# Pre-norm gains moved from the weights to the turned rows of a two-layer encoder, with queries scaled by 1/rms, two more raw weight buffers and one transfer for the constants

## The chip, the cores and the metric

The kernel runs on one core of a Trainium2 chip. The metric is the device time of one execution in microseconds (us). A core has five engines that work side by side and wait for each other by semaphores: TensorE (PE, matmuls and transposes), VectorE (DVE), ScalarE (ACT), GpSimd (POOL) and SyncE (SP, which here only issues transfers). Each takes its instructions in order.

## The reference, cut to what matters

512 rows of 1024 values pass two layers. Each layer is a token mixer with 12 query heads over 3 key/value heads, plus 4 heads that attend to 256 memory rows, then a SwiGLU network, with a norm ahead of and behind each half:

```python
def rms_norm(x, g):
    y = x * lax.rsqrt(jnp.mean(x * x, axis=-1, keepdims=True) + EPS)
    return y * g

mem_n = rms_norm(mem, mem_norm_g)
for i in range(2):
    h = rms_norm(x, g_mix_pre[i])
    proj = h @ w_in[i]                 # q (768), k (192), v (192), qm (256)
    # layer 0: window of +-128 tokens, a sink logit, rotary on 16 of 64 dims
    # layer 1: all 512 tokens; q = rope(rms_norm(q, qk_g[0])), k = rope(rms_norm(k, qk_g[1]))
    mkv = mem_n @ w_mem_kv[i]          # keys and values of the memory heads
    x = x + rms_norm(concat([tok, mo]) @ w_o[i], g_mix_post[i])
    h = rms_norm(x, g_ffn_pre[i])
    x = x + rms_norm((silu(gate) * up) @ w_down[i], g_ffn_post[i])
```

The gain `g` of a pre-norm has one value for each of the 1024 columns that a product sums over. It can be multiplied into the weights' rows, or into the activations.

## The kernel before

Everything is fp32. PE multiplies a rounded format, so every operand is split into a part `hi` and a rest `lo`, and a product is three matmuls (`mm3`, L239 to L243: hi·hi, then the two with a `lo`). `split` (L245) makes the two from a source: `hi` by ACT (or POOL, side bit 2), `lo` as source minus `hi` by DVE (or POOL, side bit 1). `split_scaled` (L257) does the same with a factor per partition.

Rows of x and of the memory are turned (transposed) by PE, so that the 1024 columns lie along the partitions: `turned` (L303) makes eight transposes of 128 x 128 into two PSUM tiles `tp` (a tag with two buffers) and splits each with one ACT and one DVE instruction of 512 columns into `hT` (x) or `mT` (memory). The factor 1/rms of a row isn't multiplied in there, but where a product is taken out of PSUM.

`unit` (L192) brings in a block of weights: a transfer into a raw buffer (`raw`, three of them), then the split, with the gain column `gcol` as the factor. There are four units of K/V weights `wkv` (768 columns), four of memory weights `wm` (1024), and per query group two of `wq` (1024). With `side` odd, POOL first multiplies `raw` by the gains in place (L214) and `split` follows; otherwise `split_scaled` does it in one go.

A mixer runs over K/V for the four row tiles (`kv_pieces`), memory keys and values (`mem_pieces`), four query groups (`q_pieces`), and then per head and row tile scores, exponentials, transposes of the probabilities and products with the values. In layer 1, `rope_b` (L398) norms keys and queries per head: squares, sum, `r` = 1/rms on POOL (L269, L270), the rotation on DVE (L414 to L416). Keys are multiplied by `r` ahead of the rotation (L409); for queries `r` is kept in `rq4` and applied later, as the scale of the exponential, for which DVE makes a bias `nb` = −max · r for every head and tile (L537). `start` (L1076) is the beginning of the program: constants, x, the four K/V units.

What sets the order: PE's is written out by hand, from a table of numbers per layer that places every piece on one axis (`put(x, f)`, L646). On the other engines and the queues a scheduler of the framework orders the instructions when the kernel is built. So PE's order is the same before and after the change, while that of ACT, DVE, POOL and SP is not.

Of the kernel before, what the change touches and what calls it, by code (L numbers as in the profile page):

```python
# [179 lines left out]
class Trunk:  # L180
    def __init__(self, tc, a):
        self.tc, self.nc, self.a = tc, tc.nc, a
# [9 lines left out]
    def unit(self, src, side=0, pool=None, parts=1, put=None, x=0, dst=None, key=None, g=None, raw=None):  # L192

# [4 lines left out]
        def load():  # L198
            raw = own or self.wraw.tile([P, 1024], F32, tag="raw", name="raw", bufs=3)
            hi, lo = [(pool or self.whl).tile([P, 1024], F32R, tag=z, name=f"w{z}", bufs=4) for z in ("hi", "lo")]  # L200
            if not own:
                nc.sync.dma_start(raw[:, :n], src)
            return raw, hi, lo

        def part(t, c0, c1):
            raw, hi, lo = t
            if g is None:
                self.split(hi[:, c0:c1], lo[:, c0:c1], raw[:, c0:c1], side)
                return
            m = n // g.shape[1]  # L210
            for k in range(c0 // m, c1 // m):
                c = slice(k * m, k * m + m)
                if side & 1:
                    nc.gpsimd.tensor_scalar(raw[:, c], raw[:, c], g[:, k:k + 1], 1.0, op0=OP.mult, op1=OP.mult)  # L214
# [42 lines left out]
    def split_scaled(self, hi, lo, src, r, pool=0):  # L257

        nc = self.nc
        if pool & 2:  # L260
            nc.gpsimd.tensor_scalar(hi, src, r, 1.0, op0=OP.mult, op1=OP.mult)
        else:
            nc.scalar.activation(hi, src, AF.Copy, scale=r)  # L263
        nc.vector.scalar_tensor_tensor(lo, src, r, hi.bitcast(F32), op0=OP.mult, op1=OP.subtract)  # L264
# [38 lines left out]
    def turned(self, h, his, los, t, nq=4):  # L303

        for b in range(2):
# [5 lines left out]
            self.split(his[k0 // nq][sl], los[k0 // nq][sl], tp)  # L311
# [30 lines left out]
    def mem_pieces(self, l, mk, put, x0, dx, lag, xw):  # L342

        w, ps = {}, []
        for u in range(4):
            self.unit(self.a["wm"][l, u], self.side(l, "mw", u), put=put, x=xw[u], dst=w, key=u,
                      g=self.gcol[:, DEPTH, 2 * u:2 * u + 2])
# [50 lines left out]
    def rope_b(self, x, t, n, z):  # L398
# [7 lines left out]
        r = self.small.tile([P, 4], F32, tag=f"r4{z}", name="r4", bufs=2 if z else 12)  # L406
        self.rstd(r[:, :n], ss[:, :n], HD)
        if z:
            v.tensor_mul(x[:, :n], x[:, :n], r[:, :n, None].to_broadcast([P, n, HD]))  # L409
# [7 lines left out]
        return r  # L417

    def rope(self, l, x, t, n, z):
        return self.rope_a(x, t, n) if l == 0 else self.rope_b(x, t, n, z)  # L420
# [40 lines left out]
    def q_pieces(self, l, c, qTs, put, x0, lead):  # L461
        nc = self.nc
        w = {}
        for z in range(2):
            self.unit(self.a["wq"][l, c, z], self.side(l, "qw", 2 * c + z), put=put, x=x0 - lead + z * lead / 3, dst=w,
                      key=z, g=self.gcol[:, l, 4 * z:4 * z + 4])

        def prod(t, st, u):
# [10 lines left out]
            if u == 3:  # L479
# [6 lines left out]
                if c < 3:  # L486
                    self.rq4[c, t] = self.rope(l, qx, t, 4, 0)
# [20 lines left out]
    def score(self, hd, i):  # L508
# [22 lines left out]
        else:  # L531
            nc.vector.tensor_reduce(nm[:, i:i + 1], s[:, :n], axis=AX.X, op=OP.max if hd["norm"] else OP.min)  # L532
        bias, scale = nm[:, i:i + 1], -1.0
        if hd["norm"]:
            r = self.rq4[hd["hg"] // 4, i][:, hd["hg"] % 4:hd["hg"] % 4 + 1]
            bias, scale = self.small.tile([P, 1], F32, tag="nb", name="nb", bufs=6), r
            nc.vector.tensor_scalar(bias, nm[:, i:i + 1], r, -1.0, op0=OP.mult, op1=OP.mult)  # L537
        nc.scalar.activation(p[:, :n], src[:, :n], AF.Exp, bias=bias, scale=scale, accum_out=den[:, i:i + 1])  # L538
# [72 lines left out]
    def consts(self, glob):  # L611
        nc, a = self.nc, self.a
        self.ropet = glob.tile([P, 2, NT, 16], F32, name="ropet")
        nc.gpsimd.dma_start(self.ropet.rearrange("p a t d -> p (a t d)"), a["ropea"])
        self.sink = glob.tile([P, NH], F32, name="sink")
        self.nsink = glob.tile([P, NH], F32, name="nsink")
        nc.gpsimd.dma_start(self.sink, _rows(a["attn_sink"], NH))
        self.gt = glob.tile([P, 2, 2, NT, HD], F32, name="gt")

    def axial(self, buf):  # L620
# [6 lines left out]
        nc.gpsimd.tensor_scalar(g[:, 0], g[:, 0], HD ** -0.5, 1.0, op0=OP.mult, op1=OP.mult)  # L627
# [7 lines left out]
    def mixer(self, l, mkp, late, tokp):  # L635
        nc = self.nc
        pc = PACE[l]
        if l == 0:
            self.mask = self.core.tile([P, 3 * P], F32, name="mask", tag="mask")
            nc.sync.dma_start(self.mask, self.a["mask"])  # L640
            nc.gpsimd.tensor_scalar(self.nsink, self.sink, -1.0, 1.0, op0=OP.mult, op1=OP.mult)
        self.pbufs = (3 * P, 15) if l == 0 else (4 * P, 12)
        qT, mk, items, count = {}, {}, [], itertools.count()
        self.rq4 = {}
# [22 lines left out]
        def heads():  # L667
            for hg in range(NH + NMH):
                c, h = divmod(hg, 4)
                hd = dict(hg=hg, norm=l == 1 and c < 3, q=lambda c=c, h=h: qT[c][:, h], sink=hg if l == 0 and c < 3 else None)  # L670
# [16 lines left out]

        k = pc["kstep"]
# [28 lines left out]
    def post_norm(self, t, og, y, e, ss, gn, resid, dst, rs, h=None):  # L717
# [17 lines left out]
        if rs is not None:  # L735
            self.factors(y, rs[:, t:t + 1], self.junk)
            return lambda: self.turned(h, *self.hT, t)
# [109 lines left out]
    def ffn_out(self, get, w, fs, o, head, gpost, resid, dst, rs):  # L847
# [25 lines left out]
        for t in range(NT):  # L873
# [5 lines left out]
            if rs is not None and t == NT - 1:  # L879
                self.wkv = [self.unit(self.a["wkv"][1, u], g=self.gcol[:, 1, 2 * u:2 * u + 2]) for u in range(4)]  # L880
# [195 lines left out]
    def start(self, mkp):  # L1076
# [3 lines left out]
        with ExitStack() as st:  # L1080
# [5 lines left out]
            nc.scalar.dma_start(ident, a["ident"])  # L1086
            self.consts(self.glob)
# [133 lines left out]
```

## Time and profile before

| | |
|---|---|
| median of 3 runs | 1134.27 us (1134.18 to 1135.16) |
| the profiled execution | 1132.73 us, its span 1131.0 us |
| granted TensorE clock, share of full speed | 0.998 |
| layer 0: K/V, memory and queries; heads | about 8 to 62 us; 63 to 180 us |
| layer 0: output of the mixer; network | to 222 us; to 537 us |
| layer 1: turning and mixer | about 555 to 745 us |
| layer 1: output of the mixer; network | to 790 us; to the end |

In the profile, a row of a timeline has the start, the duration, the engine, the line of the kernel, the operation, out<-in and shapes, how many, and in brackets the idle time ahead of it with what ended it. A row of a group has the busy us, the mean ns of one and the idle time ahead. "L255 DVE TENSOR_TENSOR hT<-tp,hT" is the `lo` part of a turned tile, for instance: the line is that of `split`, the tile tells whose it is.

### The profile page before, as it was taken

To read this page: it belongs to the slowest core of one execution; us is meant where nothing else is said; L and a number is where in the kernel's file an instruction comes from. 1 tells how busy PE (TensorE), PEld (TensorE's weight loads), DVE (VectorE), ACT (ScalarE), POOL (GpSimd) and SP (SyncE) were. 2 spreads that over 40 slices of the span, in tenths; PEclk is the share of its full clock that TensorE was granted. 3 is DMA by queue.
4 is the path that set the end of the run, shared out by engine and by line. 5 is a ranking of instruction groups with operands and counts; after the bars stand their busy time and mean duration, and the time that the engine had idled before them with its cause. 6 is when DMAs were issued, how large, how long until landed. Compare 5 with 4: busy or idle time off the path is not lost.

```text
span 1131.0 us, 19555 instructions
## 1 busy us (share of the span) xinstructions
PE 1102.3 (97%) x7463; PEld 1007.6 (89%) x7463; DVE 839.8 (74%) x1477; ACT 665.3 (59%) x1361; POOL 211.7 (19%) x370
## 2 busy tenths in 40 slices
PE   9999999999999999999999999999999999999997
PEld 7889988899889989998888888778999899899985
DVE  4788885899548857874688998758985478669854
ACT  6578984666335624553567998756654255345531
POOL 4693331102000000000327643312000000000001
PEclk9999999999999999999999999999999999999999
DMA  6521015433513332335532110145135123422243
GB/s 236 187 80 52 20 57 205 150 131 116 157 38 112 129 96 75 113 91 194 180 115 76 38 38 20 57 153 182 41 110 168 56 78 113 146 65 98 84 165 112
DMA packets 34141, 122.51 MB, mean 108 GB/s; under 512 B 3952, under 2 KB 4336, under 8 KB 33920
## 3 DMA queue, kind: packets, MB, share of 16 engines
q1 hardware_dynamic: 33696, 121.13, 32.4%
q8 instruction: 58, 0.95, 0.3%
q14 instruction: 35, 0.29, 0.1%
q0 software_dynamic: 64, 0.07, 0.1%
q10 hardware_dynamic: 288, 0.08, 0.0%
HBM read 110.77 MB, written 10.49 MB: 107 GB/s over the span
## 4 chain that ended last, share of the span: by engine, by line
PE 66%; DVE 7%; ACT 4%; POOL 2%; issue 2%; DMA 0%; POOLq 0%; DVEq 0%; ACTq 0%
PE ps L961 12%; PE ps L962 12%; PE ps L963 12%; PE ps L241 9%; PE ps L243 9%; PE ps L242 9%; PE tp L586 1%; DVE tl L255 1%; DVE wlo L264 1%; PE o L601 1%; DVE nm L532 1%; PE o L600 1%; ACT junk L274 1%; ACT p L538 1%; POOL p L576 1%
## 5 line engine op out<-in xcount | busy, mean ns | idle before, releaser
L251 ACT ACTIVATE whi<-raw 128x1024 fp32r<-128x1024 f32 (+1 forms) x176 | 148.2, 853 | 183.8 <-PE ps L963 95.8
L255 DVE TENSOR_TENSOR wlo<-raw,whi 128x1024 fp32r<-128x1024 f32 (+1 forms) x164 | 161.5, 991 | 70.6 <-ACT whi L251 70.5
L961 PE MATMUL ps<-sf,whi 128*128 128x256 f32 x640 | 180.5, 282 | 0.0
L963 PE MATMUL ps<-sf,whi 128*128 128x256 f32 x640 | 180.5, 282 | 0.0
L962 PE MATMUL ps<-sf,wlo 128*128 128x256 f32 x640 | 180.4, 282 | 0.0
L241 PE MATMUL ps<-whi,f 128*128 128x512 f32 x352 | 137.2, 390 | 0.0
L242 PE MATMUL ps<-wlo,f 128*128 128x512 f32 x352 | 137.2, 390 | 0.0
L243 PE MATMUL ps<-whi,f 128*128 128x512 f32 x352 | 137.0, 389 | 0.0
L962 PE MATMUL ps<-a,wlo 128*128 128x256 f32 x480 | 135.2, 282 | 0.0
L961 PE MATMUL ps<-a,whi 128*128 128x256 f32 x480 | 134.7, 281 | 0.0
L963 PE MATMUL ps<-a,whi 128*128 128x256 f32 x480 | 134.3, 280 | 0.0
L961 PEld LDWEIGHTS ps<-sf,whi 128*128 128x128 f32 x640 | 121.4, 190 | 0.9 <-ACT p L967 0.4
L962 PEld LDWEIGHTS ps<-sf,wlo 128*128 128x128 f32 x640 | 121.5, 190 | 0.5
L963 PEld LDWEIGHTS ps<-sf,whi 128*128 128x128 f32 x640 | 121.7, 190 | 0.0
L279 POOL TENSOR_SCALAR e<-sso 128x1 f32<-128x1 f32 x8 | 3.4, 423 | 568.9 <-ACT junk L274 568.7
L241 PE MATMUL ps<-whi,hT 128*128 128x256 f32 (+1 forms) x320 | 98.9, 309 | 0.9 <-ACT whi L263 0.9
L576 POOL TENSOR_SCALAR p<-p,rd 128x256 f32<-128x256 f32 (+2 forms) x128 | 76.8, 620 | 102.0 <-DVE rd L573 36.1
L242 PE MATMUL ps<-wlo,hT 128*128 128x256 f32 (+1 forms) x320 | 94.0, 294 | 1.0 <-DVE wlo L264 1.0
L243 PE MATMUL ps<-whi,hT 128*128 128x256 f32 (+1 forms) x320 | 93.5, 292 | 0.0
L963 PEld LDWEIGHTS ps<-a,whi 128*128 128x128 f32 x480 | 90.8, 189 | 0.0
L961 PEld LDWEIGHTS ps<-a,whi 128*128 128x128 f32 x480 | 90.6, 189 | 0.2
L962 PEld LDWEIGHTS ps<-a,wlo 128*128 128x128 f32 x480 | 90.5, 188 | 0.2
(205 smaller groups left out, 2780.5 us busy)
## 6 DMA issues: line engine op xcount, KB each, us to landing
raw<-in_wgu_dram SPq DMA_DIRECT2D x48, 512.0 KB, 4.4
raw<-in_wd_dram SPq DMA_DIRECT2D x44, 512.0 KB, 4.3
rb<-in_wgu_dram SPq DMA_DIRECT2D x40, 512.0 KB, 3.6
raw<-in_wq_dram SPq DMA_DIRECT2D x16, 512.0 KB, 3.7
raw<-in_wo_dram SPq DMA_DIRECT2D x16, 512.0 KB, 3.5
xt<-x SPq DMA_DIRECT2D x12, 512.0 KB, 4.5
raw<-in_wm_dram SPq DMA_DIRECT2D x8, 512.0 KB, 4.4
x<-y SPq DMA_DIRECT2D x8, 512.0 KB, 3.0
```

What stands on the lines that cost most here:

```text
L241: mm(out, lh, rh, start=first, stop=False)
L242: mm(out, lh, rl, start=False, stop=False)
L243: mm(out, ll, rh, start=False, stop=last)
L251: nc.scalar.activation(hi, src, AF.Copy)
L255: nc.vector.tensor_sub(lo, src, hi.bitcast(F32))
L264: nc.vector.scalar_tensor_tensor(lo, src, r, hi.bitcast(F32), op0=OP.mult, op1=OP.subtract)
L274: self.nc.scalar.activation(scratch, x, AF.Square, scale=D ** -0.5, accum_out=ss)
L532: nc.vector.tensor_reduce(nm[:, i:i + 1], s[:, :n], axis=AX.X, op=OP.max if hd["norm"] else OP.min)
L576: self.pooled = nc.gpsimd.tensor_scalar(hd["p"][z][:, :n], hd["p"][z][:, :n], rd[:, z:z + 1], 1.0, op0=OP.mult, op1=OP.mult)
L961: mm(out, wh[:, s], rh, start=start and k == 0, stop=False, skip_group_check=True)
L962: mm(out, wl[:, s], rh, start=False, stop=False, skip_group_check=True)
L963: mm(out, wh[:, s], rl, start=False, stop=k == 3, skip_group_check=True)
```

## The change

The gains are multiplied into the turned rows instead of the weights. Since after turning a column of x lies on a partition, but four of them side by side in one PSUM tile (each 128 rows wide), `turned` now splits each of the eight 128 x 128 squares by itself with `split_scaled`. Only the first tile of x is done otherwise: DVE multiplies 512 columns by a broadcast gain into a buffer, and `split` follows from there. Weights are split unscaled, in larger pieces (768 or 512 columns); POOL's scalings are gone.

In layer 1, queries are multiplied by `r` on DVE, behind the rotation (keys too, now), so the exponential's scale is −1 and its bias the score minimum `nm`; `nb` is gone. The sign is put into the query gain.

In the mixer of layer 1 two of every five raw loads use one of two new buffers (`raw2`). The identity, the rotary table of layer 0 and the gains come in one transfer `cst` on ACT's queue; the sink logits move from POOL's queue to SP's, behind x and the memory, and their negation moves into the mixer.

```diff
-    def unit(self, src, side=0, pool=None, parts=1, put=None, x=0, dst=None, key=None, g=None, raw=None):
+    def unit(self, src, side=0, pool=None, parts=1, put=None, x=0, dst=None, key=None, raw=None):
...
         def part(t, c0, c1):
             raw, hi, lo = t
-            if g is None:
-                self.split(hi[:, c0:c1], lo[:, c0:c1], raw[:, c0:c1], side)
-                return
-            m = n // g.shape[1]
-            for k in range(c0 // m, c1 // m):
-                c = slice(k * m, k * m + m)
-                if side & 1:
-                    nc.gpsimd.tensor_scalar(raw[:, c], raw[:, c], g[:, k:k + 1], 1.0, op0=OP.mult, op1=OP.mult)
-                else:
-                    self.split_scaled(hi[:, c], lo[:, c], raw[:, c], g[:, k:k + 1], side)
-            if side & 1:
-                self.split(hi[:, c0:c1], lo[:, c0:c1], raw[:, c0:c1], side)
+            self.split(hi[:, c0:c1], lo[:, c0:c1], raw[:, c0:c1], side)
...
+    def raw(self):
+
+        self.nraw += 1
+        if self.more and self.nraw % 5 in (1, 3):
+            return self.more.tile([P, 1024], F32, tag="raw2", name="raw", bufs=2)
+        return self.wraw.tile([P, 1024], F32, tag="raw", name="raw", bufs=3)
...
-    def turned(self, h, his, los, t, nq=4):
+    def turned(self, h, g, his, los, t, nq=4, buf=None):
...
-            self.split(his[k0 // nq][sl], los[k0 // nq][sl], tp)
+            hi, lo = his[k0 // nq][sl], los[k0 // nq][sl]
+            if buf is not None:
+                x = buf[:, 512 * b:512 * b + 512].rearrange("p (k n) -> p k n", n=P)
+                self.nc.vector.tensor_mul(x, tp, g[:, k0:k0 + 4, None].to_broadcast([P, 4, P]))
+                self.split(hi, lo, x)
+                continue
+            for k in range(4):
+                self.split_scaled(hi[:, k], lo[:, k], tp[:, k], g[:, k0 + k:k0 + k + 1])
...
-        if z:
-            v.tensor_mul(x[:, :n], x[:, :n], r[:, :n, None].to_broadcast([P, n, HD]))
         tmp = self.core.tile([P, 4, HD], F32, tag="rt", name="rt", bufs=2)
...
         v.tensor_add(x[:, :n], x[:, :n], tmp[:, :n])
-        return r
+        v.tensor_mul(x[:, :n], x[:, :n], r[:, :n, None].to_broadcast([P, n, HD]))
...
-            nc.vector.tensor_reduce(nm[:, i:i + 1], s[:, :n], axis=AX.X, op=OP.max if hd["norm"] else OP.min)
-        bias, scale = nm[:, i:i + 1], -1.0
-        if hd["norm"]:
-            r = self.rq4[hd["hg"] // 4, i][:, hd["hg"] % 4:hd["hg"] % 4 + 1]
-            bias, scale = self.small.tile([P, 1], F32, tag="nb", name="nb", bufs=6), r
-            nc.vector.tensor_scalar(bias, nm[:, i:i + 1], r, -1.0, op0=OP.mult, op1=OP.mult)
-        nc.scalar.activation(p[:, :n], src[:, :n], AF.Exp, bias=bias, scale=scale, accum_out=den[:, i:i + 1])
+            nc.vector.tensor_reduce(nm[:, i:i + 1], s[:, :n], axis=AX.X, op=OP.min)
+        nc.scalar.activation(p[:, :n], src[:, :n], AF.Exp, bias=nm[:, i:i + 1], scale=-1.0,
+                             accum_out=den[:, i:i + 1])
...
-            nc.scalar.dma_start(ident, a["ident"])
-            self.consts(self.glob)
-            nc.scalar.dma_start(gcol.rearrange("p z k -> p (z k)"), a["gcol"])
+            nc.scalar.dma_start(self.cst, a["cst"])
...
+            nc.sync.dma_start(self.sink, _rows(a["attn_sink"], NH))
```

How the order moves, at three places. First ACT in layer 0, at the memory tiles: `mT` is their `hi` part, `vs` and `kx` are values and keys of the last x tile on their way out of PSUM, `whi` weights. Before:

```order
L251 ACTIVATE whi<-raw 128x512 x4
L251 ACTIVATE mT<-tp 128x4x128 x2
L263 ACTIVATE vs<-ps,rs 128x3x64
L251 ACTIVATE mT<-tp 128x4x128
L263 ACTIVATE whi<-raw,gcol 128x256 x4
L444 ACTIVATE kx<-ps,rs 128x192
L251 ACTIVATE mT<-tp 128x4x128
```

After:

```order
L246 ACTIVATE whi<-raw 128x512 x4
L254 ACTIVATE mT<-tp,cst 128x128 x3
L254 ACTIVATE vs<-ps,rs 128x3x64
L254 ACTIVATE mT<-tp,cst 128x128 x2
L440 ACTIVATE kx<-ps,rs 128x192
L246 ACTIVATE whi<-raw 128x512 x2
L254 ACTIVATE mT<-tp,cst 128x128 x3
L246 ACTIVATE k_556<-kx 128x3x64
L254 ACTIVATE mT<-tp,cst 128x128 x8
```

The first memory tile had both its halves ahead of `vs`; now its eight pieces are spread around `vs`, `kx` and a weight unit, and the second tile's eight follow.

Second POOL in layer 0, from the end of the memory weights to the first normalised probabilities `p`. Before:

```order
L214 TENSOR_SCALAR raw<-raw,gcol 128x256 x8
L253 TENSOR_TENSOR wlo<-raw,whi 128x512 x2
L249 TENSOR_SCALAR whi<-raw 128x512 x2
L253 TENSOR_TENSOR wlo<-raw,whi 128x512 x2
L214 TENSOR_SCALAR raw<-raw,gcol 128x256 x3
L373 TENSOR_SCALAR k_821<-k_821 128x4x64
L214 TENSOR_SCALAR raw<-raw,gcol 128x256 x4
L249 TENSOR_SCALAR whi<-raw 128x512 x2
L373 TENSOR_SCALAR k_845<-k_845 128x4x64
L253 TENSOR_TENSOR wlo<-raw,whi 128x512 x2
L214 TENSOR_SCALAR raw<-raw,gcol 128x256 x5
L576 TENSOR_SCALAR p<-p,rd 128x256
```

After:

```order
L248 TENSOR_TENSOR wlo<-raw,whi 128x512 x4
L244 TENSOR_SCALAR whi<-raw 128x512 x2
L248 TENSOR_TENSOR wlo<-raw,whi 128x512 x2
L371 TENSOR_SCALAR k_851<-k_851 128x4x64
L244 TENSOR_SCALAR whi<-raw 128x512 x2
L371 TENSOR_SCALAR k_876<-k_876 128x4x64
L248 TENSOR_TENSOR wlo<-raw,whi 128x512 x2
L568 TENSOR_SCALAR p<-p,rd 128x256
```

Twenty scalings are gone, five of them directly ahead of `p`.

Third DVE in layer 1, at the first scores: `nm` is the score's extreme, `qx` a query tile in rotation. Before:

```order
L405 TENSOR_REDUCE ss_7461<-sq 128x4
L414 TENSOR_TENSOR rt<-qx,gt 128x4x32
L532 TENSOR_REDUCE nm<-s 128x1
L415 TENSOR_TENSOR qx<-qx,gt 128x256
L537 TENSOR_SCALAR nb<-nm,r_7196 128x1
L416 TENSOR_TENSOR qx<-qx,rt 128x256
L532 TENSOR_REDUCE nm<-s 128x1 x2
L537 TENSOR_SCALAR nb<-nm,r_7260 128x1
L537 TENSOR_SCALAR nb<-nm,r_7330 128x1
L255 TENSOR_TENSOR q_7472<-qx,q_7472 128x4x64
```

After:

```order
L403 TENSOR_REDUCE ss_7504<-sq 128x4
L410 TENSOR_TENSOR rt<-qx,gt 128x4x32
L528 TENSOR_REDUCE nm<-s 128x1
L411 TENSOR_TENSOR qx<-qx,gt 128x256
L528 TENSOR_REDUCE nm<-s 128x1
L412 TENSOR_TENSOR qx<-qx,rt 128x256
L528 TENSOR_REDUCE nm<-s 128x1
L413 TENSOR_TENSOR qx<-qx,r_7507 128x256
L528 TENSOR_REDUCE nm<-s 128x1
L250 TENSOR_TENSOR q_7516<-qx,q_7516 128x4x64
```

The small `nb` instructions are gone and a multiply of the query tile by `r` stands behind the rotation, with a score reduction and the query's `lo` part behind it.

More of the change, by code (lines that the diff above doesn't have):

```diff
@@ L198, in load @@
         def load():
-            raw = own or self.wraw.tile([P, 1024], F32, tag="raw", name="raw", bufs=3)
+            raw = own or self.raw()
             hi, lo = [(pool or self.whl).tile([P, 1024], F32R, tag=z, name=f"w{z}", bufs=4) for z in ("hi", "lo")]
@@ L345, in mem_pieces @@
         for u in range(4):
[L346 to L347 removed]
+            self.unit(self.a["wm"][l, u], self.side(l, "mw", u), put=put, x=xw[u], dst=w, key=u)
         def prod(u, m):
@@ L879, in ffn_out @@
             if rs is not None and t == NT - 1:
-                self.wkv = [self.unit(self.a["wkv"][1, u], g=self.gcol[:, 1, 2 * u:2 * u + 2]) for u in range(4)]
+                self.wkv = [self.unit(self.a["wkv"][1, u]) for u in range(4)]
             join(ps, t, 1)
@@ L1111, in factors @@
                                         op1=OP.mult)
-            self.turned(x[0], *self.hT, 0)
+            self.turned(x[0], gcol[:, 0], *self.hT, 0, buf=tmp.tile([P, D], F32, tag="buf", name="buf", bufs=1))
             busy(8)
```

57 lines of the change are left out of this document (26 added, 31 removed).

## The prediction

> **What bounds the kernel now.** I read the page first, then the waits of TensorE, then the timelines around each wait.
>
> ```profile
> span 1131.0 us, 19555 instructions
> PE 1102.3 (97%) x7463; PEld 1007.6 (89%) x7463; DVE 839.8 (74%) x1477; ACT 665.3 (59%) x1361; POOL 211.7 (19%) x370
> ```
>
> TensorE (PE) is busy 97% of the span, and neither the matmuls nor their order change. So the change is worth only what it takes from, or adds to, PE's stalls; busy time that it saves on DVE, ACT or POOL counts nowhere else. By the code it acts in the two mixers and in the turning ahead of them. The view of PE's waits, by what ended them, shows how little there is to win:
>
> ```profile
> PE tp L385 <- DVE kb L386: 2.4, 1, 2.4
> PE tp L586 <- POOL p L576: 2.0, 4, 0.9
> PE s L521 <- ACT p L538: 1.5, 2, 1.1
> PE tp L308 <- DVE mT L255: 0.9, 1, 0.9
> PE tp L586 <- DVE nb L537: 0.9, 2, 0.6
> PE o L600 <- DVE nb L537: 0.5, 1, 0.5
> ```
>
> (Columns: total us, times, longest.) These six rows together are 8.2 us, the size of the stake. Below, minus is faster.
>
> **Start of layer 0.** Four raw K/V weight units arrive, are split into hi and lo, and PE consumes them as they come:
>
> ```profile
> 9.85 1.12 ACT L263 ACTIVATE whi<-raw,gcol 128x384 fp32r<-128x384 f32 x2 [1.62 <-DMA raw<-in_wkv_dram]
> 10.51 0.45 PE L241 MATMUL ps<-whi,hT 128*128 128x384 f32 x1 [0.94 <-ACT whi L263]
> 14.28 1.03 PE L308 MATMUL tp<-ident,h 128*128 128x128 f32 x8
> ```
>
> ACT waited 1.62 us for a transfer, so the stage is set by the loads. Two software-queue transfers and one on ACT's queue go; that could let the raw units land earlier, by at most about that 1.62 us. Against it, a unit is now split in one piece of 768 instead of two of 384: with the two pieces taking 1.12 us together, PE's first matmul on a unit starts about 0.4 us later. The first x tile also makes a detour, two DVE multiplies into a buffer ahead of its split. I take **−0.3**, ends −1.0 and +0.8: the halves nearly cancel.
>
> **The turned rows in pieces.** This is what the change adds. A turned tile was two ACT and two DVE instructions of 512 columns; for the nine tiles after the first it becomes eight and eight of 128, each with its own gain column. No 128-column piece of this kind is in the trace; the nearest rows read PSUM with a per-partition scale, on ACT and on DVE:
>
> ```profile
> L251 ACT ACTIVATE hT<-tp 128x512 fp32r<-128x512 f32 x16 | 8.9, 594 | 3.6 <-PE tp L308 3.6
> L263 ACT ACTIVATE vs<-ps,rs 128x192 fp32r<-128x192 f32 x8 | 3.4, 420 | 2.7 <-PE ps L243 2.7
> L263 ACT ACTIVATE vm<-ps,rs 128x256 fp32r<-128x256 f32 x4 | 1.9, 474 | 1.3 <-DVE k L264 1.2
> L255 DVE TENSOR_TENSOR hT<-tp,hT 128x512 fp32r<-128x512 f32 x16 | 10.6, 687 | 9.0 <-ACT hT L251 8.9
> L264 DVE SCALAR_TENSOR_TENSOR vs<-ps,rs,vs 128x192 fp32r<-128x192 f32 x8 | 3.3, 411 | 0.9 <-ACT vs L263 0.7
> L264 DVE SCALAR_TENSOR_TENSOR vm<-ps,rs,vm 128x256 fp32r<-128x256 f32 x4 | 1.9, 480 | 1.6 <-ACT vm L263 1.6
> L444 ACT ACTIVATE kx<-ps,rs 128x192 f32<-128x192 f32 x8 | 3.4, 419 | 2.1 <-DVE vs L264 2.0
> ```
>
> Carrying 192 and 256 columns on to 128 gives an estimate of 0.37 us on ACT and 0.34 on DVE, so a tile takes 8 × 0.37 + 0.34 = 3.3 us from first to last instead of about 0.594 + 0.594 + 0.687 = 1.9. The last row warns of more: ACT's read of a PSUM tile waited for DVE's read of the same one, and in the changed order an ACT piece stands behind the DVE piece ahead of it, so both engines go in step and anything else queued between the pieces delays all that follow.
>
> The Trainium skill speaks against this step: "VectorE: DVE Perf Modes", section "The TRN2 errata — SBUF-src ops pay a fixed extra latency per instruction", says that every instruction pays a fixed latency and advises tiles of 512 elements or more. By its PSUM figure of 120 cycles at 0.96 GHz, an estimate for six more DVE pieces a tile is 0.75 us; the rows above agree in direction and give more, 8 × 0.34 − 2 × 0.69 = 1.3 us. With the page's price the three turning terms below (5.6 us) would shrink to some 3.2 and the sum to about −4.8, an estimate.
>
> What PE feels depends on the place.
>
> ```profile
> 15.55 1.29 DVE L255 TENSOR_TENSOR hT<-tp,hT 128x512 fp32r<-128x512 f32 x2 [0.71 <-ACT hT L251]
> 16.20 0.33 PE L241 MATMUL ps<-whi,hT 128*128 128x384 f32 x1
> 30.46 1.04 PE L308 MATMUL tp<-ident,mh 128*128 128x128 f32 x8
> 31.97 1.06 ACT L251 ACTIVATE mT<-tp 128x512 fp32r<-128x512 f32 x2
> 32.72 1.27 DVE L255 TENSOR_TENSOR mT<-tp,mT 128x512 fp32r<-128x512 f32 x2
> 33.45 1.25 PE L308 MATMUL tp<-ident,mh 128*128 128x128 f32 x8 [0.91 <-DVE mT L255]
> L274 ACT ACTIVATE scr<-h 128x512 f32<-128x512 f32 x8 | 5.0, 629 | 0.0
> ```
>
> Tile 1 of x is consumed the moment it is ready: PE begins on it at 16.20, as the first DVE half ends. PE takes some 0.5 us per column group (three matmuls of about 0.17), the pieces alone would keep up, but squares of 0.63 us and the value copy of 0.42 stand between them on ACT. Laid out in that order, the fourth column group is ready about 1.7 us after PE wants it; tiles 2 and 3 have a whole tile of products as cover. **+1.7**, ends +0.5 (squares slip into gaps) and +2.4.
>
> The memory tiles are worse. PE turns the second one at 33.45, already 0.91 us late, because it writes the PSUM tiles that the first one is still being read from. Now those come free only after pieces 7 and 8, with a value copy (0.42), a key copy and weight pieces queued between them: 31.6 for the transposes + 0.5, then 8 × 0.37 + 0.34 + 2 × 0.42 and about 1.3 of weight pieces, is 37.4. Before, the stall ended 3 us after the transposes began; now nearly 6. **+2.9**, ends +1.6 (nothing between the pieces) and +3.8 (DVE's weight pieces too).
>
> **POOL's scalings.** Each POOL-side weight unit was scaled in place first:
>
> ```profile
> L214 POOL TENSOR_SCALAR raw<-raw,gcol 128x256 f32<-128x256 f32 x36 | 18.0, 518 | 7.9 <-DMA raw<-in_wq_dram 7.8
> 69.78 2.35 POOL L214 TENSOR_SCALAR raw<-raw,gcol 128x256 f32<-128x256 f32 x5
> 72.11 2.23 POOL L576 TENSOR_SCALAR p<-p,rd 128x256 f32<-128x256 f32 x4
> 72.64 0.33 PE L586 MATMUL tp<-ident,p 128*128 128x128 f32 x1 [0.89 <-POOL p L576]
> ```
>
> At 72.64 PE waits for normalised probabilities (0.89, then 0.40 at the next), and they wait for five scalings that now are gone. Late next would be the exponentials, a little over 2 us earlier than POOL took them. **−1.8** with the slower pace of the transposes, ends −1.9 and −0.5.
>
> **Layer 1's turning.** The same pieces meet a tighter place: tile 2's transposes at 561.4 need the PSUM tiles of tile 1, and the K/V units stand among the pieces on ACT. **+1.0**, ends 0 (the 1.3 us of a tile lies beside products) and +2.3.
>
> **Layer 1's keys, queries and loads.**
>
> ```profile
> 582.01 0.73 ACT L263 ACTIVATE whi<-raw,gcol 128x512 fp32r<-128x512 f32 x1 [1.43 <-DMA raw<-in_wm_dram]
> 586.25 0.36 DVE L409 TENSOR_TENSOR kx<-kx,r 128x192 f32<-128x192 f32 x1 [1.03 <-POOL r L270]
> 587.52 0.55 DVE L386 CAST kb<-tp 128x384 fp32r<-128x384 f32 x1
> 588.22 0.43 PE L385 MATMUL tp<-identr,k 128*128 128x128 f32 x3 [2.38 <-DVE kb L386]
> 609.40 1.28 ACT L538 ACT_TABLE_LOAD   x1 [1.36 <-DVE nb L537]
> 611.62 0.50 PE L521 MATMUL s<-ka,qT 128*128 128x512 f32 x1 [1.09 <-ACT p L538]
> 612.68 1.56 POOL L214 TENSOR_SCALAR raw<-raw,gcol 128x256 f32<-128x256 f32 x3
> 616.45 1.01 POOL L270 TENSOR_TENSOR r<-r,mhalf 128x4 f32<-128x4 f32 x1
> 617.45 2.86 POOL L576 TENSOR_SCALAR p<-p,rd 128x512 f32<-128x512 f32 x4
> L537 DVE TENSOR_SCALAR nb<-nm,r 128x1 f32<-128x1 f32 x48 | 9.6, 202 | 0.2
> L415 DVE TENSOR_TENSOR qx<-qx,gt 128x256 f32<-128x256 f32 x12 | 5.2, 437 | 0.0
> ```
>
> The longest stall of all, 2.38 us, is a chain: ACT waits 1.43 for a weight transfer, so the last key tile is copied late; DVE then waits 1.03 for POOL's 1/rms; the cast of another tile, kb, is queued behind both. Two more raw buffers let that transfer start some us earlier, and the multiply by 1/rms now stands behind the rotation, which fills the wait. The waits name nothing else that would be late here: **−2.2**, ends −2.4 and 0 (the cast still stands behind the multiply).
>
> The table load no longer waits for nb, and the exponential needs the minimum alone: **−0.9** of the 1.09, ends −1.1 and 0. POOL reaches the first probabilities of layer 1 at 617.45 and hands out four in 2.86 us; PE's transposes follow at that pace of 0.72 each. Without the scalings at 612.68 POOL starts up to 1.56 earlier: **−1.4**, ends −1.6 and 0 (r, 1.01 us each time, keeps it busy instead).
>
> The 48 small DVE instructions (9.6 us) go, and twelve query multiplies of about 0.44 us (5.3) come: DVE loses 4.3 us of work in a stage where it is nearly full. The waits ended by nb are 0.9 + 0.5; those I take: **−1.4**, ends −3.0 and +1.0. Each new multiply waits in order for POOL's r, and score minima and probability lows are queued behind it.
>
> The other edits (sink's transfer and its negation, moved off the start) are at nothing: the sink is first read far behind its new place.
>
> **Sum.** −0.3 + 1.7 + 2.9 − 1.8 + 1.0 − 2.2 − 0.9 − 1.4 − 1.4 = −2.4 us. The profiled execution took 1132.73 us (1.7 around the span), so 1130.3 by its measure; the median of the runs is 1.54 above it, so **1131.9** against 1134.27. A measurement of this kernel can tell about 0.2% from no change: below 1132.0 is faster, above 1136.5 slower.
>
> **Rivals.**
> *The pieces are on the path everywhere (slower).* If, beside layer 0 at its upper ends (2.4 and 3.8), three tiles of layer 1 pay (2.3 and twice 1.2), the sum is +2.9: 1137.2. It decides once the three turning terms pass 10.3 us (8.0 of gains and the 2.3 of the bound). For it: the wait of L444 on vs above. Against it: products of the tile before as cover.
> *The pieces are hidden (much faster).* With 0.5, 1.6 and 0 for the three turning terms and 2.0 for the DVE work saved, it is −6.5: 1127.8. For it: pieces hand the first column group over sooner, and the Trainium skill's "Perfetto Trace Analysis", section "Optimizing Scalar/DVE Operations", says that breaking up instructions may complete work sooner where these engines aren't saturated. Against it: the second memory tile has no cover at all.
> *The query multiply waits for r (same).* POOL's r took 1.0 us at 616.45; if DVE stands about 0.2 us at each of the twelve and probabilities wait with it, the last two terms become −0.4 and +0.5: 1134.8.
> *The extra buffers bring nothing earlier (same).* The key stall stays: 1134.1.
>
> **Chances.** Forecast 0.40, of which 0.25 below the 0.2% bound; hidden 0.20; r 0.13; buffers 0.07; on the path 0.20. Faster 0.45, same 0.35, slower 0.20. The range, 1127.6 to 1137.0, leaves out half of each outer case.
>
> **What would show it.** Right: PE waits 2 to 4 us ahead of the second memory tile's transposes, ended by an mT piece; no waits for POOL p at 72 or 618, none of over 1 us for kb; 128-column pieces of 0.34 to 0.37 us. Wrong: pieces well over that, PE waits ended by hT in layer 1, DVE idle ended by POOL r at the query multiply, or raw units landing later.

## The result, and the profile after

| | median, us | lowest to highest |
|---|---|---|
| before, beside it | 1134.22 | 1133.03 to 1135.16 |
| after (4 runs) | 1150.35 | 1149.02 to 1151.38 |

The change makes the kernel slower: ratio 1.0142, 95% interval 1.0125 to 1.0160. The profiled execution of after took 1150.95 us.

The page of after, span and engines:

```profile
span 1149.1 us, 19543 instructions
PE 1112.8 (97%) x7463; PEld 1018.2 (89%) x7463; DVE 841.0 (73%) x1475; ACT 666.9 (58%) x1394; POOL 195.8 (17%) x327
```

The span grew by 18.2 us (1130.96 to 1149.14), but PE's busy time by 10.5 as well, with the same 7463 matmuls. So waits can't be all of it: the matmuls themselves got slower somewhere. The view of PE's waits in after (total us, times, longest) gives the other part:

```profile
PE tp L300 <- DVE mT L255: 4.7, 1, 4.7
PE tp L578 <- DVE tl L250: 4.0, 9, 1.0
PE o L592 <- DVE tok L601: 2.9, 5, 0.9
PE tp L378 <- DVE hT L255: 2.6, 2, 2.1
PE tp L300 <- DVE hT L255: 2.0, 2, 1.6
PE tp L383 <- DVE kmb L384: 1.7, 1, 1.7
...
PE tp L578 <- POOL p L568: 0.9, 2, 0.5
```

The long single waits are now ended by `hT` and `mT`, the pieces of turned rows, and by `kmb`, memory keys; kb, nb and the exponential are gone from the list. The nine waits for `tl`, the low part of the probabilities, are short. Since PE's order is unchanged, the start of one and the same matmul can be compared between the two traces, from place to place. This gives the ledger:

| stretch (us of before) | after minus before, us |
|---|---|
| start, to 15 | +0.2 |
| x tiles 1 to 3, to 31 | +5.4 |
| wait ahead of the second memory tile, at 34 | +4.1 |
| behind that wait, to 37 | +2.3 |
| first queries, 67 to 75 | +1.1 |
| layer 0 network, 233 to 550 | +1.5 |
| layer 1 turning and K/V, 550 to 584 | +2.6 |
| layer 1 mixer, to 768 | −2.8 |
| layer 1 output and network, to the last matmul | +2.9 |
| behind the last matmul (the last store lands later) | +1.0 |

The rows add up to the 18.2 us, but for rounding and −0.05 between 75 and 233 us. Three of them have no wait beside them: "behind that wait" and the two networks. The view of windows (window, us, then busy us of PE, PEld, DVE, ACT and POOL with their counts, granted clock, DMA share, GB/s) explains the first, from after:

```profile
10.88:14.29 3.41, 3.27 (x10) 3.28 (x11) 1.82 (x3) 1.34 (x4) 2.82 (x7) 0.50 1.03 417
...
30.00:32.00 2.00, 1.22 (x8) 1.22 (x9) 1.77 (x8) 1.33 (x5) 0.00 (x0) 0.84 0.00 0
32.00:34.00 2.00, 2.00 (x7) 2.00 (x7) 0.40 (x2) 0.01 (x1) 0.87 (x2) 0.50 0.02 4
34.00:36.00 2.00, 2.00 (x11) 2.00 (x11) 1.69 (x2) 0.75 (x2) 0.88 (x3) 0.81 0.00 0
...
40.00:42.00 2.00, 0.00 (x0) 0.00 (x0) 1.97 (x5) 1.27 (x4) 0.94 (x1) 0.90 0.58 229
42.00:44.00 2.00, 1.16 (x5) 0.83 (x6) 1.68 (x6) 0.63 (x3) 0.22 (x1) 0.50 0.93 279
44.00:46.00 2.00, 2.00 (x7) 1.79 (x8) 1.09 (x5) 1.42 (x5) 0.30 (x1) 0.50 0.55 195
46.00:48.00 2.00, 2.00 (x6) 1.53 (x5) 1.39 (x5) 1.19 (x4) 0.00 (x0) 0.50 0.11 43
48.00:50.00 2.00, 2.00 (x9) 1.60 (x9) 0.15 (x1) 0.51 (x1) 0.00 (x0) 0.89 0.62 262
...
82.00:84.00 2.00, 2.00 (x15) 2.00 (x14) 1.73 (x9) 1.37 (x6) 0.64 (x2) 0.64 0.00 0
84.00:86.00 2.00, 2.00 (x10) 2.00 (x10) 0.96 (x3) 1.22 (x3) 1.47 (x3) 0.51 0.00 0
```

PE is busy throughout most of these windows, at half pace: the granted clock is down to 0.50. In the first profile of before it is 1.00 over the whole of 0 to 92 us. Behind three of the new waits, all in layer 0, the matmuls run at half pace for a while, and this counts as PE's busy time; a fourth such stretch lies in the start, from 10.9 to 14.3 us. The page's row of the clock in 40 slices hides it (one digit of 8 and the rest 9).

The network is compared over the same 602 matmuls of layer 1's network; first before, then after:

```profile
1000.14:1071.14 71.00, 71.00 (x602) 71.00 (x601) 58.30 (x86) 41.58 (x70) 0.00 (x0) 1.00 0.29 97
```

```profile
1016.24:1088.23 71.99, 71.99 (x602) 71.99 (x601) 58.34 (x86) 41.52 (x70) 0.00 (x0) 1.00 0.30 96
```

No wait, the same clock, the same instructions, and 0.99 us more in 71. No line of the network is in the diff.

Last, how the long wait comes about. The pieces as groups in after:

```profile
L254 ACT ACTIVATE mT<-tp,cst 128x128 fp32r<-128x128 f32 x16 | 5.2, 364 | 3.4 <-DVE mT L255 3.1 <-PE tp L300 0.3
L255 DVE SCALAR_TENSOR_TENSOR mT<-tp,cst,mT 128x128 fp32r<-128x128 f32 x16 | 5.0, 347 | 3.8 <-ACT mT L254 3.8
```

And the timeline of after around it:

```profile
38.70 0.62 ACT L254 ACTIVATE mT<-tp,cst 128x128 fp32r<-128x128 f32 x2
39.17 0.60 DVE L255 SCALAR_TENSOR_TENSOR mT<-tp,cst,mT 128x128 fp32r<-128x128 f32 x2
39.61 1.14 ACT L246 ACTIVATE whi<-raw 128x512 fp32r<-128x512 f32 x2
39.75 1.24 DVE L391 TENSOR_TENSOR rt<-kx,cst 128x24 f32<-128x24 f32 x1
40.65 0.62 ACT L254 ACTIVATE mT<-tp,cst 128x128 fp32r<-128x128 f32 x2
42.44 0.60 DVE L255 SCALAR_TENSOR_TENSOR mT<-tp,cst,mT 128x128 fp32r<-128x128 f32 x2
42.84 2.16 PE L300 MATMUL tp<-cst,mh 128*128 128x128 f32 x8 [4.66 <-DVE mT L255]
```

The pieces are as long as estimated. But in the built program the pieces of the two PSUM tiles take turns, so that the sixth of the eight is the last of the first PSUM tile. Between the fifth and the sixth ACT slips two halves of a weight unit (1.14 us); DVE does a rotation and its own half of that unit before it takes the sixth and seventh at 42.44. The first PSUM tile comes free only then, and PE waits from 38.18 to 42.84.

### The profile page after: what moved, and what is told of

Same layout as the page of the kernel before. It is cut to its first block, busy times and chain, and to the rows that moved or that the text cites. A ratio compares the mean times of both kernels' runs of the same rounds, so it can differ in the third digit from the quotient of the medians.

```text
span 1149.1 us, 19543 instructions
## 1 busy us (share of the span) xinstructions
PE 1112.8 (97%) x7463; PEld 1018.2 (89%) x7463; DVE 841.0 (73%) x1475; ACT 666.9 (58%) x1394; POOL 195.8 (17%) x327
## 4 chain that ended last, share of the span: by engine, by line
PE 66%; DVE 7%; ACT 3%; POOL 2%; issue 1%; DMA 0%; POOLq 0%; DVEq 0%; ACTq 0%; SPq 0%
PE ps L944 12%; PE ps L946 12%; PE ps L945 12%; PE ps L236 9%; PE ps L237 9%; PE ps L238 9%; PE tp L578 1%; DVE wlo L250 1%; POOL r L261 1%; DVE nm L528 1%; PE o L593 1%; PE o L592 1%; DVE tl L250 1%; ACT p L529 1%; ACT junk L265 1%
## 5 line engine op out<-in xcount | busy, mean ns | idle before, releaser
L246 ACT ACTIVATE whi<-raw 128x1024 fp32r<-128x1024 f32 (+2 forms) x207 | 167.5, 825 | 197.4 <-PE ps L946 97.0
L250 DVE TENSOR_TENSOR wlo<-raw,whi 128x512 fp32r<-128x512 f32 (+2 forms) x198 | 187.2, 957 | 80.8 <-ACT whi L246 78.6
L944 PEld LDWEIGHTS ps<-sf,whi 128*128 128x128 f32 x640 | 122.8, 192 | 0.6
L946 PEld LDWEIGHTS ps<-sf,whi 128*128 128x128 f32 x640 | 122.8, 192 | 0.0
L236 PE MATMUL ps<-whi,hT 128*128 128x256 f32 (+1 forms) x320 | 101.0, 316 | 1.2 <-ACT hT L246 0.7
L238 PE MATMUL ps<-whi,hT 128*128 128x256 f32 (+1 forms) x320 | 95.8, 299 | 0.2 <-DVE hT L250 0.2
L944 PEld LDWEIGHTS ps<-a,whi 128*128 128x128 f32 x480 | 92.1, 192 | 0.2
L946 PEld LDWEIGHTS ps<-a,whi 128*128 128x128 f32 x480 | 92.1, 192 | 0.0
```

Of the source, the lines that this page charges most:

```text
L236: mm(out, lh, rh, start=first, stop=False)
L238: mm(out, ll, rh, start=False, stop=last)
L246: nc.scalar.activation(hi, src, AF.Copy)
L250: nc.vector.tensor_sub(lo, src, hi.bitcast(F32))
L944: mm(out, wh[:, s], rh, start=start and k == 0, stop=False, skip_group_check=True)
L946: mm(out, wh[:, s], rl, start=False, stop=k == 3, skip_group_check=True)
```

## The experiments

The theory after the result: the pieces cost nearly all of it, partly as waits and partly through the clock behind them, and the networks' slower pace comes from something else that the change moves. The rivals: the clock and the networks are chance, or the mover is the query multiply, the loads or the extra buffers. The runs of before beside these kernels had medians of 1134.3 to 1134.5.

**Is it chance?** Before once more, unchanged.

> The kernel before, unchanged, profiled again on the chip that runs the others. Theory A (the 16 us come from the first 90 us and from layer 1's mixer): its network stages have the same pace as those of the changed kernel here, about 12.0 us per hundred of the 256-column matmuls. Rival B (the change slows the networks too): they run at 11.85 to 11.9 again while the changed kernel's run at 12.0.

1134.94 us, and the networks ran at the pace of the first profile (start differences to it +1.43 at 233 us and +1.43 at 550, +2.21 at 768 and +2.19 at the end). The slower networks are no chance of one execution. The differences themselves lie mostly at two stretches of half clock, 12.6 to 16.0 and 589.4 to 592.8 us, which the first profile of the same kernel doesn't have: whether one follows a wait varies between executions.

**Pieces alone, on the kernel before.** Gains stay in the weights; only the split of a turned tile is cut in pieces, four to each PSUM tile (for all ten turned tiles; the change leaves the first one whole):

```diff
-            self.split(his[k0 // nq][sl], los[k0 // nq][sl], tp)
+            hi, lo = his[k0 // nq][sl], los[k0 // nq][sl]
+            for k in range(4):
+                self.split(hi[:, k], lo[:, k], tp[:, k])
```

> The kernel before with one edit: each turned tile is split in eight pieces of 128 columns, unscaled, in both layers. Theory A: the pieces alone cost most of the loss, 1142 to 1150 us, with a wait of 3 us or more ahead of the second memory tile and a granted clock under 1.0 right after it. Rival B: up to 1137.

1147.42 us, ratio 1.0113 [1.0096, 1.0130]: the pieces alone cost 13.1 us. PE's waits in this kernel:

```profile
PE tp L308 <- DVE mT L255: 5.5, 1, 5.5
...
PE tp L382 <- DVE hT L255: 2.0, 1, 2.0
```

The same two places, with the clock at 0.50 behind both; by 37 us of before the delay is 11.6 us, layer 1's turning adds 2.4, and the networks add nothing. So the pieces are shown to be the greater part (the first tile, 1.2 us late by 15 us, is in this figure but not in the change), and shown not to be what slows the networks.

**Whole tiles instead of pieces, in layer 0, on the kernel after.** DVE multiplies 512 columns into a buffer, as for the first tile, and `split` follows; layer 1 keeps its pieces:

```diff
-                x = buf[:, 512 * b:512 * b + 512].rearrange("p (k n) -> p k n", n=P)
+                x = buf().rearrange("p (k n) -> p k n", n=P)
...
-                late[t] = lambda t=t: (self.turned(x[t], gcol[:, 0], *self.hT, t), factors(t, scr))
+                late[t] = lambda t=t: (self.turned(x[t], gcol[:, 0], *self.hT, t, buf=buf), factors(t, scr))
```

(and the same for the memory tiles; `buf` is one tile of 512 columns, which all the halves share).

> The changed kernel, but in layer 0 and for the memory every turned tile goes the way of the first: two DVE multiplies of 512 columns into a buffer, then one split each; layer 1 keeps its pieces. Theory A (pieces of 128, between which other work of ACT and DVE stands, hold the PSUM tiles and starve TensorE): most of the 12 us that layer 0 lost by 50 us come back, 1140 to 1143 us. Rival B (constants, larger weight units or a slower network stage): 1148 to 1151.

1144.85 us, 1.0096 [1.0081, 1.0111], between the two expectations: 5.5 us come back, not 7 to 10. The clock stayed at 1.00 through the memory tiles, but the third pass over each half tile is a cost too; waits take the place of waits:

```profile
PE ps L238 <- DVE hT L250: 2.9, 2, 2.8
...
PE tp L300 <- DVE buf L306: 1.7, 1, 1.7
```

**Is the half clock a cost of its own?** The kernel after, with 40 useless matmuls of 128 columns put ahead of the second memory tile's transposes. The order on ACT, DVE and POOL stays the same; they only keep PE active in the gap:

```diff
+            def fill(n):
+                if n:
+                    z = self.tagged("pv")
+                    for _ in range(n):
+                        nc.tensor.matmul(z[:, :P], self.identr, self.identr, start=True, stop=True)
...
-                late["m", m] = lambda m=m: (self.turned(mh[m],
+                late["m", m] = lambda m=m: (fill(40 * m), self.turned(mh[m],
```

> The changed kernel with 40 more matmuls of 128 columns, of no use to the result, on TensorE ahead of the second memory tile's transposes, where it waits 4.8 us. Theory A (after a long idle stretch the granted clock falls to a half for some us, and that doubles the price of the wait): the filler keeps TensorE active, the memory products after 43 us run at 0.23 instead of 0.43 us, 2 to 3 us less: 1147 to 1148.5 us. Rival C (the matmuls are slow after the wait because of their operands or for another reason): no change, 1149 to 1151.5.

1147.89 us, 1.0118 [1.0103, 1.0133]: 2.5 us less than after, for more work on PE, and all four executions (1145.98 to 1148.85) lie below the four of after. The two windows in which the clock was 0.50 now read:

```profile
44.00:46.00 2.00, 1.96 (x11) 1.68 (x12) 1.20 (x5) 1.22 (x5) 0.46 (x1) 1.00 0.71 242
46.00:48.00 2.00, 2.00 (x10) 1.63 (x9) 1.49 (x5) 1.57 (x5) 0.00 (x0) 1.00 0.11 39
```

The ledger's +2.3 "behind that wait" is down to 0.5, while the wait's own cost stays (the second memory tile's transposes begin 9.54 us late, 9.39 in after). So a wait of PE here has two prices, its length and the half clock behind it.

**What slows the networks?** The change also takes small tiles out of SBUF: six of `nb`, and eleven of fourteen `r4`. In the built programs the raw, split and network buffers that lie behind them begin at byte 12288 of a partition before and at 11744 after; 12288 is a multiple of 128, 11744 lies 32 above a multiple of 64. So the kernel after was run with one unused tile of 32 bytes ahead of them (11776), and the kernel before with one of 96 bytes (12384, also 32 above a multiple of 64). Nothing else was edited:

```diff
             self.small = self.pool(top, "small")
+            self.small.tile([P, 8], F32, name="pad")
```

> The changed kernel with 32 bytes of unused SBUF per partition in the pool ahead of the weight buffers, no instruction changed. The removed small tiles (nb, r4) had moved the raw, hi, lo and hT buffers from addresses that are multiples of 128 bytes to 96 above one; the pad puts them back on multiples of 128. Theory D (the address of the operands sets the pace of the network's 256-column matmuls: 120.0 ns each in the changed kernel, 118.2 to 119 in the one before): the pace goes back, 4 to 4.5 us less, 1145.5 to 1146.5 us. Rival E (the pace comes from another part of the change, such as the transfers or the order on ACT and DVE): no change, 1149 to 1151.5.

> The kernel before with 96 bytes of unused SBUF per partition at the same place, which puts its weight and hT buffers at 96 above a multiple of 128 bytes, as in the changed kernel; no instruction changed. Theory D: its networks slow to 120.0 ns a matmul, 1138 to 1139 us. Rival E: 1134 to 1135.

The pads leave the order of instructions on every engine as it was. After with the pad: 1.0109 [1.0094, 1.0125], with 1145.85, 1147.02 and 1147.24 us, some 3.5 us less than after; one further execution, that with the profile, took 6156 us and is left out. Before with the shift: 1136.62 us, 1.0021 [1.0012, 1.0030], 2.4 us more than before, and less than expected. The padded kernel was run once more for the missing profile:

> The kernel of e5_pad once more, for its profile, which a disturbed execution had spoilt. Theory D: the 256-column matmuls of both networks mix 116, 118, 120 and 122 ns again, mean 118.2 to 119. Rival E: 120.0.

1143.66 us, lower than the three above. Its 602 matmuls, then those of the shifted kernel before:

```profile
1010.13:1081.12 70.99, 70.99 (x602) 70.99 (x601) 58.32 (x86) 41.55 (x70) 0.00 (x0) 1.00 0.30 97
```

```profile
1002.20:1074.19 71.99, 71.99 (x602) 71.99 (x601) 58.33 (x86) 41.55 (x70) 0.00 (x0) 1.00 0.29 96
```

The pace follows the address in both directions, on kernels whose networks are the same code. In the padded kernel both networks are back at the pace of before (differences of 0.0 between 233 and 550 us and from 768 us to the last matmul, where after lost 1.5 and 2.9). What the address does inside the chip isn't shown, and the shift isn't the mirror image of the pad: the shifted kernel lost 2.2 in the second stretch, but only 0.1 in the first.

**The rest of the change, without turned pieces.** The kernel after with the gains back in the weights (and POOL's scalings with them) and buffers at a multiple of 128:

> The change without its first part and with the 32 bytes of pad: the gains stay in the weights (scaled by ACT, DVE and POOL as before), turned tiles are split in 512 columns; the queries' multiply by 1/rms, the two raw buffers and the single transfer of constants are in. Theory A (the loss is turning in pieces, plus the addresses): 1130 to 1133.5 us, better than both kernels, with the wait of 2.4 us for kb gone. Rival F (the remaining parts cost too, by DVE's waits for POOL's r in layer 1): 1134.5 to 1137.

1132.80 us, 0.9988 [0.9979, 0.9997]. So constants, query multiply and raw buffers together are a small gain. From here to the padded kernel after it is 14 us: this is what moving the gains cost as a whole, little more than the pieces alone (13.1).

**Which part of the rest?** Three kernels: e7 without the two raw buffers; before with only the queries (and keys) multiplied by 1/rms on DVE; before with only the constants in one transfer and the sink on SP's queue.

> The run e7_rest without the two extra raw buffers. If they are worth what the forecast gave them (2.2 us at the wait for kb): 1134.5 to 1135.5. If the wait for kb is ended by something else anyway, as POOL's third key copy did in e7_rest: 1132.5 to 1133.5.

1133.34 us, 0.9994 [0.9985, 1.0002]: the buffers are worth 0.5 us, within what can be told. PE's waits without them and then with them (e7):

```profile
PE tp L392 <- DVE kmb L393: 4.3, 2, 4.0
```

```profile
PE tp L392 <- POOL k L380: 2.0, 1, 2.0
```

The wait for kb is gone in both, so it was not the buffers that ended it; another, also at key transposes, stands in its place: of 4.0 us at 614 without the buffers, of 2.0 us at 589 with them. (The buffers alone on the kernel before weren't tried: SBUF is 32 bytes short for them.)

> The kernel before with one part of the change: in layer 1 queries and keys are multiplied by 1/rms on DVE behind the rotation, the exponential takes the score minimum as it is. 32 bytes of pad keep the buffers on multiples of 128 bytes. Theory I (my forecast for this part): about 3 us less, 1131 to 1132. Rival J (DVE waits in order for POOL's r at the new multiply, with probability lows and token adds queued behind, and gives back what it saved): 1134 to 1136.

1136.16 us, 1.0020 [1.0011, 1.0029]: the part loses 1.9. Its profile shows why, at the memory keys and first queries of layer 1:

```profile
608.50 2.70 POOL L253 TENSOR_TENSOR wlo<-raw,whi 128x512 fp32r<-128x512 f32 x2
...
612.47 1.02 POOL L270 TENSOR_TENSOR r<-r,mhalf 128x4 f32<-128x4 f32 x1
...
613.52 0.42 DVE L415 TENSOR_TENSOR qx<-qx,r 128x256 f32<-128x256 f32 x1 [2.87 <-POOL r L270]
614.86 0.68 DVE L386 CAST kmb<-tp 128x512 fp32r<-128x512 f32 x1
...
615.68 0.72 PE L385 MATMUL tp<-identr,k 128*128 128x128 f32 x4 [3.97 <-DVE kmb L386]
```

POOL is splitting weights, so `r` is late; DVE stands 2.87 us at the query multiply; the cast of the memory keys (`kmb`) is queued behind it, and PE waits 3.97 for that cast. Against the first profile of before, the same matmuls start 2.4 us earlier behind 588 us than they did ahead of it (the wait for kb is gone, with the key multiply moved and without other buffers), 3.0 us earlier at 612, and 3.8 us later at 618: the new wait takes back more than the old one gave. Of these 6.8 us some 2.6 come behind the wait, where the granted clock is 0.50 from 615.0 to 621.8.

> The kernel before with one part of the change: identity, rotary table and gains in one transfer on ACT's queue, the sink on SP's queue behind x and the memory. Weight buffers stay on multiples of 128 bytes. Theory G (POOL's software-queue transfer of the sink, 384-byte pieces, holds back the second to fourth K/V weight unit by 1.8 us): those units land at 8.0, 9.0 and 9.9 us instead of 10.0, 10.9 and 11.9, the stalls of the first 14 us shrink, 1131.5 to 1132.8 us. Rival H (layer 0's next wait takes it back): 1133.5 to 1134.5.

1131.74 us, 0.9976 [0.9966, 0.9986]: faster than both kernels. The view of transfers in the first 12 us (issues, KB each, median us from issue to landing), before and then this kernel:

```profile
raw<-in_wkv_dram SPq DMA_DIRECT2D x4, 384.0 KB, 8.0
```

```profile
raw<-in_wkv_dram SPq DMA_DIRECT2D x4, 384.0 KB, 6.0
```

and its second x tile is turned at

```profile
12.11 1.03 PE L308 MATMUL tp<-cst,h 128*128 128x128 f32 x8
```

instead of 14.28. The four K/V units, on another queue, land 2.0 us earlier, and PE is 2.2 us earlier from there to 33 us, and 1.6 to 1.8 from then to 584. Which of the two edits does it, the single transfer or the sink's place, isn't told apart.

Last, whether a multiple of 64 bytes is enough: the same kernel with a pad of 64 bytes (12352).

> The run e9_const with 64 bytes of unused SBUF ahead of the weight buffers, which then lie 64 above a multiple of 128 bytes; no instruction changed. If multiples of 64 are enough for the faster pace of the 256-column matmuls (theory D, weak form): 1131 to 1132.5 us, as e9_const. If it takes multiples of 128 (or more): pace towards 119.5 to 120 ns, 1133.5 to 1136.

1131.25 us, 0.9969 [0.9958, 0.9980], the lowest median of all, and not to be told from the kernel without the pad. Its 602 matmuls:

```profile
997.96:1069.16 71.20, 71.20 (x602) 71.20 (x601) 58.31 (x86) 41.58 (x70) 0.00 (x0) 1.00 0.30 97
```

**The parts together.** The rest of the change takes the kernel to 1132.8, moving the gains adds some 14, and the addresses some 3.5, which is after's 1150.35. These are differences along one row of kernels, so they must add up and prove nothing by it. Values found apart agree with them: the pieces alone 13.1; constants −2.5, query multiply +1.9 and buffers −0.5, together −1.1, against −1.5 for the three in one kernel.

## Why the prediction was wrong

The forecast was 1131.9 us and the upper end 1137.0; the time lies 13 above that end.

**The turned rows in pieces** failed, by size: the three terms were +1.7, +2.9 and +1.0, and the ledger has +5.4, +6.4 (4.1 and 2.3) and +2.6. Half pace is 1.5 of the first, read off the start differences between 30.8 and 34.6 us of after, and about 2.1 of the second (2.6 behind the wait, less the 0.5 that stays with the filler). The 3.9, 4.3 and 2.6 that are left are each above the upper ends of 2.4, 3.8 and 2.3. The duration of a piece was right (0.364 and 0.347 against 0.37 and 0.34), and the slip in the sum for the memory tiles (37.5, not 37.4) is small. Three steps behind it were wrong.
- For x it said "tiles 2 and 3 have a whole tile of products as cover". The pieces share ACT and DVE with squares, value copies and weight units, and the delay was handed on from tile to tile. After the last tile's products PE stood 2.12 us ahead of the key transposes.
- For the memory tiles it priced what ACT had queued, 1.3 us of weight pieces. It put DVE's own half of those weights into the upper end only, and DVE's sixth piece was the one that decided.
- It had no price for the clock. The half pace behind the waits was in no term, no bound and no rival, though the view of windows has a column for it.

**The rival with the pieces on the path** had the right mechanism and sign. Its price, 1137.2, added upper ends that were too low for the same reasons.

**The networks** were at nothing by silence: "neither the matmuls nor their order change", so only stalls could count. Their addresses change, because tiles ahead of them go; this is 4.4 us of the ledger (1.5 and 2.9, with layer 1's output in the second), and about 3.5 by the runs with pads. That the change takes away small tiles was read as saved work only.

**The start**, −0.3: one half was much too low. Fewer transfers are worth −2.5 by themselves, beyond the bound of −1.0 (the 1.62 us of one wait were taken for all that the loads could give). In after's profile it is gone by 15 us (+0.2), for two reasons. Half clock from 10.9 to 14.3 us is one: the padded kernel, with the same instructions and the clock at 1.00 there, is 1.3 us ahead of before at this place, 1.5 more than after. What else is missing (1.3 against the 2.2 of the kernel with the transfers alone) goes with the larger weight pieces and the first tile's detour, which no run separates.

**POOL's scalings at 72**, −1.8: the wait for `p` is gone, and the delay falls by 1.7 us at the two transposes that waited for it; how much of this is only PE's own lateness isn't told apart. But ahead of them the wait for kmb grew from 0.36 to 1.67 us, and half pace behind it cost 1.5, so that the row of the ledger is +1.1.

**Layer 1's keys, queries and loads**, −5.9 in all: −2.8. The waits for kb, nb and the exponential are gone as forecast; the first and the last gave 2.5 and 1.1 us at their places. Of the two reasons given for kb one wasn't needed: without the raw buffers, which are worth 0.5 by the runs, the wait is gone too, with the moved key multiply. The −1.4 for probabilities at 618 didn't come: PE's waits for `p` between 585 and 640 us were 0.7 and are 0.9. In place of nb's 1.4 us, PE's waits for `tl`, which DVE makes, grew to 4.0 us in the whole of after (3.3 in layer 1, where they were 0.8), from this row of before:

```profile
PE tp L586 <- DVE tl L255: 1.5, 4, 0.8
```

And the rival in which the query multiply waits for `r` holds: alone the part costs 1.9. In after, with POOL free of scalings, it is milder; DVE's waits there between 600 and 760 us:

```profile
DVE qx L413 <- POOL r L261: 2.5, 5, 0.9
```

## What to carry to other kernels

Before cutting a PSUM reader into pieces, list what else both engines have queued, since the tile is held until the last piece of the slower one; and price a wait of a busy PE twice, by its length and by the clock in the windows behind it; the second price falls due in some executions and not in others. When an edit removes or adds small tiles, compare the start addresses of the large matmul operands before and after, and measure once with a pad. Nothing that PE waits for should be queued behind a multiply that itself waits for a slow engine's small result. And a clean-up of the first loads is worth trying by itself.

## What the runs showed of the hardware that was not expected

**Clock behind short waits.** The stretches at half clock behind waits in after last 3.4 us from 31.4 on, 6.8 from 41.6 on and 3.4 from 82.6 on, behind waits of 2.12, 4.66 and 1.67 us. The Trainium skill, "TensorE: Matmul & The Clock Gate", section "Why this matters for your kernels", advises no PE gaps over about 3 us. The lengths fit the window of about 3.4 us that the page names in Part 1, but two of the three drops came behind shorter waits. The length alone doesn't decide: of two executions of before, one had half clock behind the wait for kb and one hadn't. The traces show what does. All changes of the clock in one trace lie whole multiples of 3.413 us apart, so time is cut into windows of that length, and the clock of a window goes with PE's idle time in the one ahead of it. In the first profile of before the wait for kb lies across the edge of two windows (the first two rows, 1.32 and 1.06 us idle), in the second execution within one (the next two, 2.08):

```profile
583.75:587.16 3.41, 2.09 (x20) 1.94 (x18) 2.31 (x5) 2.80 (x7) 1.49 (x2) 1.00 0.68 203
587.16:590.57 3.41, 2.35 (x21) 2.38 (x22) 3.41 (x12) 0.74 (x2) 0.81 (x3) 1.00 0.45 139
586.00:589.41 3.41, 1.33 (x13) 1.22 (x13) 2.38 (x8) 1.68 (x4) 1.26 (x2) 1.00 0.79 264
589.41:592.82 3.41, 3.41 (x18) 3.41 (x19) 3.38 (x10) 0.75 (x2) 1.57 (x3) 0.50 0.55 150
```

Over the 13 traces (all but that of 6156 us), up to 1100 us and from windows at full clock, each of the 13 with 1.86 us idle or more was followed by 0.50, and none of those with 1.36 or less; between the two both happened.

**Matmul pace by address.** With buffers 32 bytes above a multiple of 64, the 602 matmuls took 71.99 us in two kernels; at multiples of 64 or 128 they took 70.99 to 71.20 in three. The rule isn't complete: with the pad of 64 bytes layer 0's network (233 to 550 us) was 1.0 us faster than in before, which no other kernel was.

**Two engines beside each other.** DVE's rotation of 24 columns took 1.24 us at 39.75 in after, while POOL was in a split; the same one took 0.18 at 30.12, with POOL idle:

```profile
30.12 0.18 DVE L391 TENSOR_TENSOR rt<-kx,cst 128x24 f32<-128x24 f32 x1
...
35.97 4.98 POOL L248 TENSOR_TENSOR wlo<-raw,whi 128x512 fp32r<-128x512 f32 x4 [1.12 <-ACT whi L246]
```

It ended 0.04 us behind that split. In the padded kernel, with the same instructions in the same order, the rotation met the split later, took 0.59 and ended 0.04 behind it again, and PE's wait was 4.00 us instead of 4.66. In the kernel with whole tiles POOL was idle at this rotation, and it took 0.17. So POOL's split had a part in the long wait; no run was made for this alone.
